# Holding back the feed-forward weight loads of a decoder layer until a given load of the second output projection

## The chip, the cores and the metric

One core of one Trainium2 chip runs the whole program. The metric is the device time of one execution in microseconds (us); the time before is the median of three runs. Engines: PE is the matmul engine and PEld its weight load, DVE, ACT and POOL are the vector, scalar and GpSimd engines, and SP issues the DMAs.

## The reference

One decoder layer, batch 1, 1024 tokens, model width 1024, float32. The token mixer has two halves of 512 columns, an RWKV-7 recurrence over 8 heads and a causal convolution of width 31, from one input projection `w_in` to one output projection `w_out`. A gated feed-forward network with a causal convolution of width 3 and an inner width of 2816 follows.

```python
h = _rms_norm(x, norm_pre_mix)
p = h @ w_in                     # 2 x 512 convolution columns, then the RWKV columns
...                              # recurrence, head norm, gate; convolution, norm, silu
mix = jnp.concatenate([rwkv_out, c], axis=-1) @ w_out
x = x + _rms_norm(mix, norm_post_mix)
h = _rms_norm(x, norm_pre_ffn)
hid = _causal_dwconv(h @ ffn_up, ffn_conv_w, ffn_conv_b)
gate, up = hid[..., :D_FF], hid[..., D_FF:]
x = x + _rms_norm((gelu(gate) * up) @ ffn_down, norm_post_ffn)
```

## The kernel before

**Weights.** Every large product is done in three matmuls on a rounded high part and a low part: high by high, high by low and low by high. `Trunk.weight` makes such a pair. It loads a 128 x 512 block (256 KB) into a raw buffer `wr` on SP's queue (line 180), ACT rounds it to `wh` and POOL subtracts to get `wl` (both on line 166, a helper). Line 139 is the helper of every matmul and line 154 that of the transposes on PE, so tiles tell more than lines: `pb`, `pe`, `pc`, `xs` and `Y` are PSUM banks, `h` the normed input of the mixer in two parts, `f` that of the feed-forward network, `wm` a pair of `w_out`.

**Order.** The code is written as streams with priorities, and a scheduler puts each engine's instructions into one fixed order. An engine runs its own in that order, and an instruction that waits holds up all behind it. `weight` runs at high priority, so a load whose buffer is free goes to the front of the order. SP has eight DMA semaphores in turn: each DMA waits until the one eight before it has landed. `tc.issue_after(i)` allows the instruction inside it only behind instruction `i` in that order; the kernel has it in a few places.

**Raw buffers.** The feed-forward phase takes its raw buffers in turn from two pools: two from `wq`, then three from `wp`. Those of `wq` hold nothing in the mixer.

**Stages.** First the program loads rows of `x` (`l8`), `params` (370 columns of per-channel constants), and the `lora` weights. Each row block is normed (lines 302 to 323: a sum of squares on ACT, its root on POOL at line 161, the scaling on ACT and DVE), transposed on PE, and written as `h` with a per-channel factor out of `params` (ACT line 288, DVE line 290). The first projection follows. The sequence is done in two halves of 512 tokens, and the recurrence in four quarters. Between about 20 and 655 us projection, recurrence, convolution and nine early pairs of feed-forward columns run interleaved. `norm_ffn(0)` in that stretch makes `f` of the first half: a sum of squares on ACT into `pt` (line 880), a factor `kk` on DVE (line 887), matmuls of `kk` with the row, then ACT line 288 and DVE line 290. The recurrence of the same stretch inverts small triangular matrices in a chain on DVE (`sub` and `dw`, lines 602 and 604). The second output projection `w_out(1)` ends the mixer at about 675 us. It has four column blocks `ch` of 256, each with four loads `k2`. The rest is the feed-forward network.

Of the kernel before, what the change touches and what calls it, by code (L numbers as in the profile page):

```python
# [100 lines left out]
class Trunk:  # L101
    def __init__(self, ctx, tc, a):
        self.ctx, self.tc, self.nc, self.a = ctx, tc, tc.nc, a
        self.at = dict(PRIO)
        self.n = 0

        self.low_pool = True

        once = [None]
        self.homes = {"wr": cycle(once), "wh": cycle(once), "wl": cycle(once)}  # L110

    def nm(self, s):
# [61 lines left out]
    def weight(self, src, shape, home=None, held=None, kept=None):  # L174


        with self.tc.high_priority():
            raw = (self.f2p.tile(shape, F32, tag="f2", name=self.nm("wr")) if held is self.hp else
                   self.wtile("wr", shape))
            self.load = self.nc.sync.dma_start(raw, src)  # L180
            if held:
                hi, lo = self.pair("w", held)
            elif home:
                hi, lo = (home[0].tile(shape, F32R, tag=t, bufs=BUFS[t], name=self.nm("wm")) for t in home[1:])
            else:
                hi, lo = (self.wtile(t, shape, F32R) for t in ("wh", "wl"))
            if kept and kept[0]:
                self.nc.scalar.copy(hi, raw)  # L188
                self.nc.sync.dma_start(lo.bitcast(F32), kept[1])
            else:  # L190
                self.low = self.split(hi, lo, raw, self.low_pool)[1]
        if kept and not kept[0]:
            self.nc.sync.dma_start(kept[1], lo.bitcast(F32))
        return hi, lo
# [579 lines left out]
    def w_out(self, h, mixr, co, behind=None):  # L774
        nc = self.nc
        if h == 0:
            acts = self.pairs("m")
        else:
            acts = []
            for _ in range(2):  # L780
                two = [self.tl("l8", [P, 4, HALF], F32R) for _ in range(2)]
                acts += [tuple(b[:, k] for b in two) for k in range(4)]
        with ExitStack() as gate:
            if behind is not None:
                gate.enter_context(self.tc.issue_after(behind.ins))
            for k in range(KT):
                self.split(*acts[k], mixr[:, k] if k < 4 else co[k - 4])

        def evac(ch, pss, post):
            for b, ps in enumerate(pss):  # L790
                o = self.tl("t2", [P, 512])
                with self.tc.high_priority():
                    nc.vector.tensor_tensor(
                        o.rearrange("p (t c) -> p t c", t=2), ps.rearrange("p (t c) -> p t c", t=2),
                        post.unsqueeze(1).broadcast_to([P, 2, 256]), ALU.mult)
                    for t in range(2):
                        tt = 4 * h + 2 * b + t
                        c = slice(t * 256, (t + 1) * 256)
                        nc.scalar.activation(ps[:, c], ps[:, c], AF.Square, accum_out=self.ssq[:, tt, ch:ch + 1])  # L799
                r = h * HALF + b * 256  # L800
                nc.sync.dma_start(
                    self.mixd[r:r + 256, ch * 256:(ch + 1) * 256].rearrange("(t p) c -> p t c", t=2),
                    o.rearrange("p (t c) -> p t c", t=2))

        for ch in range(4):
            post = self.tl("po", [P, 256])
            nc.sync.dma_start(post, self.a["post_mix"][:, ch * 256:(ch + 1) * 256].broadcast_to([P, 256]))
            pss = self.xs if ch == 1 else [self.bank("pe" if h and ch == 2 else "pb") for _ in range(2)]
            for k2 in range(KT // 2):
                wh, wl = self.weight(self.a["w_out"][ch, k2], [P, 2, 256], (self.mix, "ca", "ck") if h else None)  # L810
                for t in range(4):
                    for kk in range(2):
                        k = 2 * k2 + kk
                        hi, lo = acts[k]
                        s = slice(t * P, (t + 1) * P)
                        out = pss[t // 2][:, (t % 2) * 256:(t % 2 + 1) * 256]
                        start = k == 0 and t % 2 == 0
                        i = self.mm(out, hi[:, s], wh[:, kk], start=start, stop=False, skip=True)
                        if start:
                            first = i  # L820
                        elif k == 0 and kk == 0:
                            self.after(i, first)
                        self.mm(out, hi[:, s], wl[:, kk], start=False, stop=False, skip=True)
                        self.mm(out, lo[:, s], wh[:, kk], start=False, stop=k == KT - 1, skip=True)
            evac(ch, pss, post)


    def setup_ffn(self, ctx):
# [429 lines left out]
    def mixer(self, sts):  # L1258
        nc, tc = self.nc, self.tc
        W = [None] * 4  # L1260
        mixes = [None] * 2
# [141 lines left out]
                nc.sync.dma_start(self.early[i], self.ffn_pair(0, h0, i, piece, two[:, i % 2 * HALF:(i % 2 + 1) * HALF]))  # L1403
        prepare(4)
        with self.stream("proj"):
            self.w_out(1, mixes[1], [sts[1]["co", i] for i in range(4)], W[3].merged)
        return h0


# [71 lines left out]
```

## Time and profile before

| | |
|---|---|
| median of 3 runs | 1265.08 us |
| lowest and highest | 1264.17 and 1265.79 us |
| profiled execution | 1266.88 us |
| its span | 1265.1 us |
| mean granted PE clock | 0.984 |
| PE busy | 1216.0 us of the span |
| DVE, ACT, POOL busy | 901.4, 730.6, 512.2 us |
| moved by DMA | 180.97 MB, mean 143 GB/s |

The profiled execution has its own time: 1.8 us lies around its span, and it stands 1.8 us above the median. "Idle" is time in which an engine has no instruction in flight, and the bracket at the end of a row gives the idle time ahead of it and what ended it. The granted clock of PE is given in tenths of full speed (9 in a slice is 90% or more) or as a mean.

### The profile page before, as it was taken

The numbers are of one execution on the slowest core, as the hardware profiler recorded it, in microseconds if no ns is written. First come the engines' busy times: TensorE is split into PE (matmuls) and PEld (weight loads), VectorE is DVE, ScalarE is ACT, GpSimd is POOL, SyncE is SP. The second block draws the span as 40 slices with busy tenths as digits, with TensorE's granted clock in tenths as the row PEclk, the third lists the DMA queues.
The fourth block names the chain that finished last, engine by engine and source line by source line (L and its number), as shares of the span: only waits on it lengthen the run. The fifth ranks groups of instructions, "written<-read, shape, count | busy, mean of one in ns | idle before, by whom it ended". The sixth has DMA issues, their size and how long they took to land.

```text
span 1265.1 us, 22976 instructions
## 1 busy us (share of the span) xinstructions
PE 1216.0 (96%) x8424; PEld 993.7 (79%) x8424; DVE 901.4 (71%) x1558; ACT 730.6 (58%) x1516; POOL 512.2 (40%) x447
## 2 busy tenths in 40 slices
PE   5999999999998998999999999999999999999997
PEld 4767777788777876778889888888888888888885
DVE  6275999798678978999640455666766669479668
ACT  6564564564954676465763476876556556545451
POOL 3443330002103332244464389998889860000002
PEclk9999997999999989999999999999999999999998
DMA  7644442344332354133354698995232335336413
GB/s 254 172 133 141 127 133 71 90 126 126 111 119 80 110 157 137 44 88 90 100 141 147 226 333 288 305 319 165 79 84 77 93 127 179 100 104 225 133 56 133
DMA packets 102912, 180.97 MB, mean 143 GB/s; under 512 B 14896, under 2 KB 21424, under 8 KB 102800
## 3 DMA queue, kind: packets, MB, share of 16 engines
q1 hardware_dynamic: 102800, 179.51, 45.2%
q8 instruction: 66, 1.08, 0.4%
q14 instruction: 46, 0.38, 0.1%
HBM read 138.44 MB, written 41.03 MB: 142 GB/s over the span
## 4 chain that ended last, share of the span: by engine, by line
PE 78%; DVE 10%; ACT 5%; issue 2%; DMA 2%; POOL 2%; SPq 0%; POOLq 0%; DVEq 0%; ACTq 0%
PE pb L139 39%; PE xs L139 17%; PE pe L139 16%; DVE pc L427 3%; PE Y L139 2%; PE pc L139 2%; POOL wl L166 1%; PE pe L154 1%; DVE dw L604 1%; DMA pt<-mixd 1%; DMA params<-params 1%; DVE pt L496 1%; PE pc L154 1%; DVE sub L602 1%; PE xs L154 0%
## 5 line engine op out<-in xcount | busy, mean ns | idle before, releaser
L166 POOL TENSOR_TENSOR wl<-wr,wh 128x512 fp32r<-128x512 f32 (+2 forms) x175 | 233.7, 1337 | 226.0 <-ACT wh L166 188.9
L139 PE MATMUL pb<-h,wh 128*128 128x512 f32 (+3 forms) x720 | 231.4, 402 | 2.1 <-ACT wh L166 1.4
L166 ACT CAST wh<-wr 128x512 fp32r<-128x512 f32 (+1 forms) x214 | 131.3, 615 | 132.8 <-PE pb L139 42.8
L139 PE MATMUL pb<-f,wh 128*128 128x512 f32 x648 | 203.2, 393 | 0.7 <-ACT pb L799 0.4
L427 DVE SCALAR_TENSOR_TENSOR pc<-c,params,pc 128x512 f32<-128x512 f32 x232 | 174.2, 751 | 7.5 <-ACT pc L424 3.4
L139 PEld LDWEIGHTS pb<-h,wh 128*128 128x128 f32 (+2 forms) x720 | 133.0, 191 | 34.8 <-ACT wh L166 3.3
L139 PE MATMUL pb<-h,wl 128*128 128x512 f32 (+3 forms) x360 | 146.6, 407 | 2.1 <-POOL wl L166 2.0
L139 PEld LDWEIGHTS pb<-f,wh 128*128 128x128 f32 x648 | 120.9, 188 | 26.1 <-issue 1.0
L139 PE MATMUL pb<-f,wl 128*128 128x512 f32 x324 | 128.0, 396 | 0.0
L161 POOL TENSOR_TENSOR ss<-var,mhalf 128x1 f32<-128x1 f32 x16 | 11.6, 732 | 222.7 <-DVE var L160 222.6
L1069 POOL TENSOR_TENSOR b<-b,b 128x512 f32<-128x512 f32 x72 | 93.4, 1300 | 2.0 <-DMA wr<-ffn_up 0.6
L139 PEld LDWEIGHTS pb<-h,wl 128*128 128x128 f32 (+2 forms) x360 | 68.6, 190 | 21.1 <-POOL wl L166 4.2
L139 PE MATMUL xs<-f,wh 128*128 128x512 f32 x240 | 74.1, 390 | 0.3 <-DVE act L966 0.3
L166 POOL TENSOR_TENSOR wl<-b,wh 128x512 fp32r<-128x512 f32 x48 | 67.1, 1398 | 13.4 <-ACT wh L166 11.6
L139 PEld LDWEIGHTS pb<-f,wl 128*128 128x128 f32 x324 | 60.8, 188 | 12.9 <-POOL wl L166 0.4
L139 PE MATMUL pe<-f,wh 128*128 128x512 f32 x208 | 64.1, 389 | 0.0
L166 ACT CAST wh<-b 128x512 fp32r<-128x512 f32 x48 | 29.7, 618 | 57.4 <-PE pb L139 17.1
L717 POOL TENSOR_TENSOR XG<-r,GE 64x256 f32<-64x256 f32 x30 | 20.6, 690 | 80.2 <-DVE r L736 58.9
L139 PEld LDWEIGHTS xs<-f,wh 128*128 128x128 f32 x240 | 44.9, 188 | 9.9 <-DVE act L966 0.8
L166 ACT CAST a<-act 128x512 fp32r<-128x512 f32 x50 | 30.0, 619 | 33.4 <-PE Y L139 18.9
L188 ACT CAST wh<-wr 128x512 fp32r<-128x512 f32 (+2 forms) x44 | 26.4, 603 | 37.5 <-PE pb L139 21.0
L166 ACT CAST w<-wr 128x512 fp32r<-128x512 f32 x38 | 23.5, 622 | 41.3 <-PE Y L139 20.0
(419 smaller groups left out, 2965.9 us busy)
## 6 DMA issues: line engine op xcount, KB each, us to landing
wr<-ffn_up SPq DMA_DIRECT2D x99, 256.0 KB, 3.3
wr<-w_in SPq DMA_DIRECT2D x80, 256.0 KB, 2.9
b<-ffn_up SPq DMA_DIRECT2D x52, 256.0 KB, 2.7
b<-ffn_down SPq DMA_DIRECT2D x44, 256.0 KB, 4.6
sums<-b SPq DMA_DIRECT2D x44, 256.0 KB, 4.0
wr<-sums SPq DMA_DIRECT2D x44, 256.0 KB, 2.8
lows<-wl SPq DMA_DIRECT2D x40, 256.0 KB, 3.3
wl<-lows SPq DMA_DIRECT2D x40, 256.0 KB, 2.7
```

Of the source, the lines that this page charges most:

```text
L139: return self.nc.tensor.matmul(out, lhsT, rhs, start=start, stop=stop, skip_group_check=skip)
L154: self.nc.tensor.transpose(out, in_, self.con("ident")[:n, :n])
L161: self.nc.gpsimd.tensor_tensor(out, v[:, :n], self.mhalf[:, :n], ALU.pow)
L166: return self.nc.scalar.copy(hi, src), eng.tensor_tensor(lo, src, hi.bitcast(F32), ALU.subtract)
L188: self.nc.scalar.copy(hi, raw)
L427: nc.vector.scalar_tensor_tensor(out, c[:, j:j + HALF], w(j), acc, ALU.mult, ALU.add)
L496: nc.vector.tensor_tensor_scan(sg[:, l], self.con("scan"), sg[:, l], 0.0, ALU.mult, ALU.add)
L602: nc.vector.tensor_tensor(tv, dv[:, j + 1:, j:j + 1].broadcast_to([P, n, j]), dv[:, j:j + 1, :j].broadcast_to([P, n, j]), ALU.mult)
L604: nc.vector.tensor_tensor(dv[:, j + 1:, :j], dv[:, j + 1:, :j], tv, ALU.add)
L717: nc.gpsimd.tensor_tensor(x[64:128], R[64:128, gs], w.GE[64:128, c, gs].unsqueeze(2).broadcast_to([64, 4, CH]), ALU.mult)
L1069: sub = lambda o, x, y, op=ALU.subtract: self.nc.gpsimd.tensor_tensor(o, x, y, op)
```

## The change

`weight` gets a gate: once `self.start` is set, each of its loads may stand only behind that instruction. `w_out` keeps the load that its second column block begins with, and the mixer sets `self.start` to that of the second output projection. The loads of the mixer itself, of `w_out` and of the nine early pairs are made while `start` is still `None`; all loads that `weight` makes later are of the feed-forward network.

```diff
@@ Trunk.__init__
+        self.start = None
@@ Trunk.weight
-            self.load = self.nc.sync.dma_start(raw, src)
+            with ExitStack() as gate:
+                if self.start is not None:
+                    gate.enter_context(self.tc.issue_after(self.start.ins))
+                self.load = self.nc.sync.dma_start(raw, src)
@@ Trunk.w_out
                 wh, wl = self.weight(self.a["w_out"][ch, k2], ...)
+                if ch == 1 and k2 == 0:
+                    mark = self.load
...
+        return mark
@@ mixer
-            self.w_out(1, mixes[1], [sts[1]["co", i] for i in range(4)], W[3].merged)
+            self.start = self.w_out(1, mixes[1], [sts[1]["co", i] for i in range(4)], W[3].merged)
```

On SP at the start of the program, three loads of `ffn_up` stand among the first loads before. Behind the rows of `x`, SP has before:

```order
L302 DMA l8_4_129<-x 128x512 x4
L180 DMA wr_1194_7921<-ffn_up 128x512
L180 DMA wr_1197_7940<-ffn_up 128x512
L213 DMA params_78<-params 128x370
L214 DMA const_79<-consts 128x449
L244 DMA lora_106<-lora 96x512
L248 DMA wr_1_109<-lora 128x512
L248 DMA wr_2_113<-lora 128x512
L180 DMA wr_46_274<-w_in 128x512
L302 DMA mixr_111_679<-x 128x512 x4
L302 DMA ck_112_680<-x 128x512
L180 DMA wr_1219_8045<-ffn_up 128x512
```

and now:

```order
L306 DMA l8_4_129<-x 128x512 x4
L217 DMA params_78<-params 128x370
L218 DMA const_79<-consts 128x449
L248 DMA lora_106<-lora 96x512
L252 DMA wr_1_109<-lora 128x512
L252 DMA wr_2_113<-lora 128x512
L184 DMA wr_46_274<-w_in 128x512
L306 DMA mixr_111_679<-x 128x512 x4
L306 DMA ck_112_680<-x 128x512
L306 DMA ck_113_681<-x 128x512
```

The three loads are gone from there. With them the split of the first leaves ACT (`wh_1195`) and POOL (`wl_1196`): on POOL it stood ahead of the root of the last row block. Before:

```order
L161 TENSOR_TENSOR ss_32_212<-var_35_218,mhalf_83 128x1
L166 TENSOR_TENSOR wl_1196_7924<-wr_1194_7921,wh_1195_7923 128x512
L161 TENSOR_TENSOR ss_36_223<-var_38_229,mhalf_83 128x1
L251 TENSOR_TENSOR lw_108<-wr_1_109,lw_108 32x512
L251 TENSOR_TENSOR lw_108<-wr_2_113,lw_108 32x512
```

and now:

```order
L162 TENSOR_TENSOR ss_32_212<-var_35_218,mhalf_83 128x1
L162 TENSOR_TENSOR ss_36_223<-var_38_229,mhalf_83 128x1
L255 TENSOR_TENSOR lw_108<-wr_1_109,lw_108 32x512
L255 TENSOR_TENSOR lw_108<-wr_2_113,lw_108 32x512
L167 TENSOR_TENSOR wl_48_277<-wr_46_274,wh_47_276 128x512
```

The root `ss_36` now follows the one before it at once. At the second output projection ACT's casts of the feed-forward weights stand elsewhere. Before:

```order
L166 CAST wm_1112_7403<-wr_1111_7401 128x512
L166 CAST l8_1100_7319<-co_902_6129 128x512
L166 CAST wh_1198_7942<-wr_1197_7940 128x512
L923 ACT_TABLE_LOAD
L923 ACTIVATE pt_1068_6992<-pt_1068_6992 128x512
L166 CAST wm_1115_7433<-wr_1114_7431 128x512
L903 ACTIVATE pt_1076_7034<-pb_1069_6997,params_78 128x512
L905 COPY ecarry_93<-pb_1069_6997 128x2
L166 CAST wm_1121_7475<-wr_1120_7473 128x512
```

and now:

```order
L167 CAST wm_1112_7403<-wr_1111_7401 128x512
L930 ACT_TABLE_LOAD
L930 ACTIVATE pt_1068_6992<-pt_1068_6992 128x512
L167 CAST wm_1115_7433<-wr_1114_7431 128x512
L910 ACTIVATE pt_1076_7034<-pb_1069_6997,params_78 128x512
L912 COPY ecarry_93<-pb_1069_6997 128x2
L167 CAST wm_1121_7475<-wr_1120_7473 128x512
L167 CAST wh_1195_7923<-wr_1194_7921 128x512
L167 CAST wh_1198_7942<-wr_1197_7940 128x512
L167 CAST wm_1124_7505<-wr_1123_7503 128x512
```

Here `wr_1120` is the load that the gate names, and the two casts `wh_1195` and `wh_1198` have moved behind its cast; on SP the loads `wr_1194` and `wr_1197` follow `wr_1120` directly.

The order in the middle of the mixer is not the same either, though no line of its code is changed. On all engines it is the same from about row 50 up to the work that runs at about 170 us before, and again from the end of `w_out(1)`; between, the scheduler has placed many instructions a few rows up or down, and ACT has one table load fewer in all. The place of the largest shift that the prediction speaks of is `norm_ffn(0)` next to the recurrence, on ACT. Before:

```order
L590 COPY l8_792_5305<-l8_792_5305 32x32x32
L288 ACTIVATE f_880_5988<-pb_887_6019,params_78 128x256
L288 ACTIVATE f_882_5990<-pb_887_6019,params_78 128x256
L726 COPY r_833_5518<-xs0_100 64x256
L567 COPY ck_809_5431<-pe_808_5426 128x512
L567 COPY ck_811_5438<-pe_810_5433 128x512
L880 ACTIVATE pt_894_6050,sf_858_5939<-row_892_6044 128x512
L726 COPY r_833_5518<-xs1_101 64x256
L567 COPY ck_813_5445<-pe_812_5440 128x512
L567 COPY ck_815_5452<-pe_814_5447 128x512
```

and now:

```order
L887 ACTIVATE pt_894_6050,sf_858_5939<-row_892_6044 128x512
L292 ACTIVATE f_880_5988<-pb_887_6019,params_78 128x256
L292 ACTIVATE f_882_5990<-pb_887_6019,params_78 128x256
L594 COPY l8_792_5305<-l8_792_5305 32x32x32
L730 COPY r_833_5518<-xs0_100 64x256
L730 COPY r_833_5518<-xs1_101 64x256
L571 COPY ck_809_5431<-pe_808_5426 128x512
L571 COPY ck_811_5438<-pe_810_5433 128x512
L292 ACTIVATE f_868_5976<-pb_896_6060,params_78 128x256
```

The last sum of squares `pt_894` stands six rows higher, and the factors of `f` behind it (`f_868`) follow before `ck_813`. On DVE the second half of `f` stands now ahead of most of the chain of `sub` and `dw`:

```order
L606 TENSOR_TENSOR sub_818_5467<-dw_103 128x26
L608 TENSOR_TENSOR dw_103<-dw_103,sub_818_5467 128x13x2
L294 SCALAR_TENSOR_TENSOR f_869_5977<-pb_896_6060,params_78,f_868_5976 128x256
L294 SCALAR_TENSOR_TENSOR f_871_5979<-pb_896_6060,params_78,f_870_5978 128x256
L740 TENSOR_TENSOR r_843_5829<-xs0_100,XG_844_5838 64x256
L606 TENSOR_TENSOR sub_819_5470<-dw_103 128x36
```

Before, `f_869` stood three steps of that chain later, behind the `dw` of `sub_821`.

## Prediction

> **What bounds the kernel now.** I read the busy lines and the clock of the page first, then busy time by stretch, for where PE has time to win.
>
> ```profile
> PE 1216.0 (96%) x8424; PEld 993.7 (79%) x8424; DVE 901.4 (71%) x1558; ACT 730.6 (58%) x1516; POOL 512.2 (40%) x447
> PEclk9999997999999989999999999999999999999998
> 0.00:20.00 20.00, 7.85 (x30) 5.58 (x31) 11.41 (x34) 13.51 (x30) 8.21 (x15) 1.00 0.89 296
> 20.00:40.00 20.00, 18.48 (x88) 15.09 (x87) 9.74 (x29) 11.56 (x25) 7.82 (x10) 1.00 0.51 170
> 300.00:340.00 40.00, 39.62 (x305) 30.99 (x304) 27.82 (x55) 28.81 (x58) 6.51 (x10) 1.00 0.36 112
> 480.00:500.00 20.00, 17.21 (x218) 14.63 (x218) 17.66 (x43) 12.05 (x30) 4.73 (x6) 0.91 0.45 150
> 500.00:520.00 20.00, 16.52 (x110) 13.01 (x106) 17.45 (x52) 10.43 (x24) 2.89 (x5) 0.91 0.05 16
> 640.00:660.00 20.00, 18.83 (x125) 17.07 (x124) 11.48 (x14) 14.55 (x29) 15.47 (x12) 1.00 0.58 151
> 720.00:1240.00 520.00, 520.00 (x2311) 430.44 (x2310) 353.99 (x552) 313.50 (x639) 277.40 (x217) 1.00 0.52 168
> ```
>
> In the rows of stretches the columns are start and end, length, then busy time of PE, PEld, DVE, ACT and POOL, the granted clock, and the DMA engines' share and GB/s. PE is the bound: from 720 to 1240 us it has no idle time, and its order there is unchanged, so nothing can be won or lost in that stretch. PE is idle for 12.15 us at the start, where the DMA engines are 89% busy, 1.52 us in the next 20, 1.17 us around 650, and 6.3 us from 480 to 520, at a lower clock. The change touches these places.
>
> **The start.** Here is the chain of work that ended last for the first 30 us (start, length, what), then rows of the timeline, then two of the DMA view of the first 26 us.
>
> ```profile
> 4.97 0.57 SPq L180
> 6.20 7.10 DMA params<-params
> 13.32 5.39 DMA mixr<-x
> 18.77 4.99 DMA wr<-w_in
> 23.79 0.63 ACT wh L166
> 24.48 1.28 POOL wl L166
> 25.80 5.95 PE pb L139 x34
> ```
>
> ```profile
> 11.56 0.62 ACT L166 CAST wh<-wr 128x512 fp32r<-128x512 f32 x1 [0.33 <-DMA wr<-ffn_up]
> 12.61 1.28 POOL L166 TENSOR_TENSOR wl<-wr,wh 128x512 fp32r<-128x512 f32 x1
> 13.39 0.84 ACT L288 ACTIVATE h<-pe,params 128x256 fp32r<-128x256 f32 x2
> 13.84 0.79 POOL L161 TENSOR_TENSOR ss<-var,mhalf 128x1 f32<-128x1 f32 x1
> 21.18 0.77 PE L139 MATMUL pb<-h,wh 128*128 128x256 f32 x2 [0.48 <-DVE h L290]
> 24.46 0.80 PE L139 MATMUL pb<-h,wh 128*128 128x256 f32 x2 [0.38 <-ACT wh L166]
> 25.80 0.58 PE L139 MATMUL pb<-h,wl 128*128 128x256 f32 x1 [0.55 <-POOL wl L166]
> 28.74 0.63 PE L139 MATMUL pb<-h,wh 128*128 128x256 f32 x2
> 29.78 0.40 PE L139 MATMUL pb<-h,wh 128*128 128x256 f32 x2
> 15.40 0.33 SPq L180 DMA_DIRECT2D wr<-ffn_up  x1
> 31.66 0.62 ACT L166 CAST wh<-wr 128x512 fp32r<-128x512 f32 x1 [0.82 <-PE pb L139]
> ```
>
> ```profile
> GB/s 0 0 32 158 334 321 277 303 265 221 277 202 230 388 407 403 398 405 358 232 286 271 347 388 391 384 384 391 391 378 391 388 355 347 383 397 375 224 69 3
> wr<-ffn_up SPq DMA_DIRECT2D x3, 256.0 KB, 6.6
> ```
>
> The chain runs through the first of two `ffn_up` issues ahead of `params`, then through transfers that queue behind each other, to the second `w_in` pair, for which PE waits twice: 0.38 us for `wh` at 24.46 and 0.55 us for `wl` at 25.80. The GB/s row cuts those 26 us into 40 slices, and from the 23rd on it stands at about 388. A load of 256 KB (0.262 MB) takes 0.262 / 388 GB/s = 0.68 us of that.
>
> The change removes two loads ahead of `params` and a third, issued at 15.40, ahead of the second `w_in` load. So `params` lands 2 x 0.68 = 1.35 us sooner, and that `w_in` block 3 x 0.68 = 2.0 us, since each DMA of SP waits for one that landed earlier by as much. ACT starts on `h` 0.1 us after `params` at 13.39; it loses the 0.62 us cast at 11.56, and POOL the 1.28 us subtraction, behind which the root at 13.84 had waited. ACT is busy from there to the first projection, so I take only the 0.62 us cast for the start of PE: 21.18 becomes 20.6. Both waits for the second pair then vanish, because `wl` is ready at 25.76 - 2.0 = 23.7, before PE asks at 25.80 - 0.60 - 0.38 - 0.55 = 24.27. The work that starts at 25.80 starts 1.53 us sooner.
>
> One price is not in the trace: PE runs at half rate here (0.63 us for two matmuls at 28.74, 0.40 us at 29.78, while the clock column says 1.00). If the full rate comes at the same moment as before, nothing is added. If it comes about 4 us after the last stall, as before (25.80 to 29.4), with no stall after 20.6 it comes at about 24.6, and the 4.8 us until 29.4 shrink by half, 2.4 us. I add 0.9 of that, below the middle because the DVE chain at 21 us may stall PE again: 2.4 us for the start, with bounds 0.6 (only the cast goes) and 3.9.
>
> [...]
>
> **The second output projection.** Two casts move on ACT, and three loads on SP's queue, into this stretch.
>
> ```profile
> 649.58 0.63 ACT L166 CAST wh<-wr 128x512 fp32r<-128x512 f32 x1
> 652.72 0.38 PE L139 MATMUL pb<-wm,l 128*128 128x256 f32 x1 [0.31 <-ACT wm L166]
> 653.96 0.50 PE L139 MATMUL xs<-wm,l 128*128 128x256 f32 x2 [0.86 <-ACT wm L166]
> 654.30 7.25 PE L139 MATMUL pb<-wm,l 128*128 128x256 f32 x59
> ```
>
> ACT is the engine that PE waits for, 0.31 + 0.86 us. The cast of `wh_1198` at 649.58 lies in ACT's chain ahead of those waits and moves behind `wm_1121`, a gain of up to 0.63 us. Against that, `wm_1124` now has two casts of 0.63 us ahead of it, and these wait for loads issued only behind `wr_1120`. PE then has 7.25 us of matmuls, from 654.30 on, that need none of them, and the loads, 3 x 0.68 us, fill a queue that is 58% busy. SP's two later `ffn_up` loads wait for a buffer that POOL frees, with `w_out` loads queued behind; those have the same cover. I take a gain of 0.3 us, bounds -0.6 and +1.3 (both casts exposed).
>
> **The middle.** The gate moves nothing there itself, but the scheduler's order changed with the times it assumes. Most of it lies where PE has nothing to win: from 300 to 340 us, where ACT loses a table load, PE is idle for 0.38 us of 40. I put this at nothing, covered by PE's own queue; its bound is one half-clock stretch of 3.4 us either way, 1.7 us. The largest shift is in `norm_ffn(0)`.
>
> ```profile
> 501.69 0.27 PE L139 MATMUL xs<-r,ck 128*64 128x64 f32 x1 [1.17 <-ACT r L726]
> 502.62 0.65 ACT L880 ACTIVATE pt<-row 128x512 f32<-128x512 f32 x1
> 505.75 0.28 DVE L887 TENSOR_SCALAR kk<-const,sf 128x128 f32<-128x128 f32 x1
> 510.25 3.30 PE L139 MATMUL pb<-kk,row 128*128 128x128 f32 x16 [2.03 <-DVE sub L602]
> 513.78 0.89 PE L139 MATMUL pb<-f,wh 128*128 128x512 f32 x2 [0.23 <-DVE sub L602]
> 509.24 0.87 DVE L290 SCALAR_TENSOR_TENSOR f<-pb,params,f 128x256 fp32r<-128x256 f32 x2
> 518.81 1.16 DVE L612 STREAM_TRANSPOSE dw<-dw 64x512 f32<-64x512 f32 x1
> ```
>
> The chain is `pt` at 502.62, `kk` at 505.75, PE, then the four `f` pairs of DVE, the first at 509.24, for which PE's second batch waited 2.03 us; the `sub` named there stood ahead on the same engine. From 513.78 on PE has feed-forward work in plenty. ACT's `pt` now stands ahead of two `f`, two `ck` copies and a copy of `r`, about 2.5 us sooner, so PE's waits of 1.17, 2.03 and 0.23 us, together 3.4 us, can be filled by recurrence work that stood ahead of them. I take half, 1.7 us, because that work depends on ACT and DVE too. Bounds: 3.4 gained, plus one half-clock stretch that ends with the idle, 1.7, so 5.1; or as much as 3.5 lost, below.
>
> **The sum.** The profiled execution took 1266.88 us (span 1265.1). 2.4 + 0.3 + 1.7 = 4.4 us gives 1262.5 for it. It stands 1.8 us above the median of 1265.08, so I forecast 1260.7.
>
> **Rivals.**
>
> *Gained at the start, given back (within 0.2%, 2.5 us, which is about what a measurement of this kernel can tell from no change).* The shift of 1.5 us arrives at a stage that waits for something else. For it speaks the idle time of PE at 480 to 520 us, where DVE is busy for 17.66 and 17.45 us of 20 and could be the one that sets the pace; against it, that work on the weights, such as the cast at 31.66, is released by PE itself and shifts along. Start 1.5, middle nothing: 1265.1 - 1.5 = 1263.6.
>
> *Slower by the inversion.* On DVE eight `f` of 0.44 us (0.87 for two) now stand ahead of the chain of `sub` and `dw` that ends in the transpose at 518.81. If PE and ACT are late with the second batch, DVE waits at these `f` and the chain ends later by 3.5 us and more. It decides from the point at which PE runs out of feed-forward matmuls behind 513.78. Then PE waits 3.5 us, one half-clock stretch adds 1.7, and a second one elsewhere in the reordered mixer 1.7 more: 1265.1 - 2.4 + 6.9 = 1269.6, or 1267.9 without the last.
>
> *Faster by the start alone.* The clock comes early, the middle stays as it is: 1265.1 - 3.9 + 0.3 = 1261.5 to 1262.
>
> *The gate stalls the transition.* ACT waits at `wh_1195` for its load and PE runs dry before `wm_1124`: +1.3 us, 1263.8 with the start's gain. PE's 7.25 us of cover speak against it.
>
> **Chances.** The sum 0.40 and the start alone 0.14, so 0.54 faster; given back 0.19 and stalled transition 0.06, so 0.25 the same; the inversion or its like 0.21 slower. The range takes in the start at its bound with the middle at its own (1265.1 - 3.9 - 0.6 - 4 = 1256.6) and above it the inversion at its lower price: 1256.5 to 1267.5. That leaves out a fifth: the inversion's dearer half and the sums of all the best bounds.
>
> **What would show it.** In the changed kernel `params` should land near 12 us, the first projection start near 20.6, PE show no wait for the second `w_in` pair, and two matmuls of 128x256 fall to 0.40 us near 25 to 28 instead of 29.6. At 640 to 660 PE should wait less than 1.17 us, with `wm_1124` cast before PE needs it. At 500 to 520 PE should be busy for more than 16.52 us. If PE's time at the end of `w_out(1)` is not 3 us or more sooner, the middle took the gain; a longer chain of `sub` and `dw` with PE waiting for `dw` behind it would be the inversion.

## The result, and the profile after

The changed kernel takes 1253.91 us (median of six runs, 1252.75 to 1257.58) against 1265.43 us of the kernel before beside it (1264.06 to 1266.73): a ratio of 0.9913 with an interval of 0.9897 to 0.9929, 11.5 us faster. The forecast was 1260.7 us, and its range ended at 1256.5. The profiled execution took 1257.58 us, the slowest of the six, with a span of 1255.8 us; against the profiled one of before, 1265.1 us, it shows 9.3 of the 11.5 us.

These are the busy line, the clock line and the stretches of the changed kernel, with the columns as in the prediction.

```profile
PE 1210.4 (96%) x8424; PEld 988.9 (79%) x8424; DVE 899.8 (72%) x1558; ACT 729.1 (58%) x1515; POOL 507.1 (40%) x447
PEclk9999998999999989999999999999999999999999
0.00:20.00 20.00, 8.46 (x32) 5.98 (x32) 11.00 (x36) 13.50 (x31) 6.81 (x14) 1.00 0.90 299
20.00:40.00 20.00, 18.79 (x99) 14.76 (x99) 8.58 (x27) 11.46 (x25) 9.15 (x10) 1.00 0.52 152
300.00:340.00 40.00, 39.04 (x278) 29.86 (x277) 29.50 (x56) 32.27 (x67) 6.75 (x11) 1.00 0.39 118
428.00:455.00 27.00, 25.61 (x340) 23.37 (x339) 26.12 (x41) 19.42 (x49) 10.81 (x10) 1.00 0.47 134
480.00:500.00 20.00, 16.91 (x175) 13.22 (x173) 19.28 (x50) 16.52 (x40) 3.61 (x6) 1.00 0.20 70
500.00:520.00 20.00, 19.57 (x312) 15.86 (x314) 19.07 (x39) 8.54 (x16) 7.06 (x6) 0.91 0.19 48
640.00:660.00 20.00, 20.00 (x166) 19.91 (x165) 3.73 (x5) 9.20 (x22) 14.49 (x11) 0.99 0.75 220
720.00:1240.00 520.00, 520.00 (x2311) 430.70 (x2310) 353.63 (x560) 306.11 (x623) 276.17 (x216) 1.00 0.51 164
```

The stretch of 428 to 455 us was not shown of before; it is there:

```profile
428.00:455.00 27.00, 22.91 (x340) 20.82 (x339) 25.08 (x40) 19.17 (x41) 7.07 (x7) 0.89 0.44 113
```

PE is idle there for 4.09 us before and 1.39 us after, and the granted clock goes from 0.89 to 1.00. From 720 us on nothing has changed, as forecast. Stretches by the clock hide a shift, because work has moved against them. So the table takes one PE matmul, the same in both kernels, at each of ten places, and gives how much sooner (minus) it starts than in the kernel before; the first line is its time before. It is worked out from the traces.

| us before | 40 | 272 | 380 | 392 | 410 | 428 | 455 | 527 | 639 | 663 |
|---|---|---|---|---|---|---|---|---|---|---|
| changed kernel | -3.4 | -4.5 | -4.1 | -2.9 | -5.7 | -6.4 | -12.9 | -13.7 | -12.6 | -9.3 |
| `start_only` | -1.4 | -1.1 | -1.1 | -1.1 | -1.1 | -1.1 | -2.0 | -3.6 | -4.1 | -4.7 |
| `order_only` | -1.2 | -2.3 | -2.0 | -0.7 | -3.5 | -4.2 | -10.8 | -12.4 | -12.9 | -9.8 |
| `stage3a` | -1.8 | -3.3 | -3.3 | -3.3 | -3.3 | -4.0 | -11.3 | -9.8 | -9.8 | -10.3 |
| `pool_slot` | -1.2 | -1.1 | -1.1 | -1.1 | -3.8 | -3.8 | -3.8 | -4.7 | -4.8 | -5.5 |
| `evac_pe` | -2.0 | -2.0 | -2.0 | -2.0 | -2.0 | -2.0 | -7.3 | -5.2 | -5.0 | -5.8 |
| `combo` | -2.1 | -4.0 | -4.0 | -4.0 | -6.7 | -7.4 | -14.7 | -16.6 | -17.2 | -14.6 |

In the changed kernel 3.4 us are won by 40 us, 2.8 from 392 to 410, 6.5 from 428 to 455, and 3.3 are lost from 639 to 663. The two gains in the middle stand at places to which the prediction gave nothing. One trace is one execution, and the start differs by 1.3 us among kernels with one order there (in the eight gated ones with the old order the first 128x512 matmul starts at 28.87 to 30.18 us); the verdicts below go by medians.

### The profile page after: what moved, and what is told of

Its sections match the earlier page's. It is cut to its first block, busy times and chain, and to the rows that moved or that the text cites. A ratio compares the mean times of both kernels' runs of the same rounds, so it can differ in the third digit from the quotient of the medians.

```text
span 1255.8 us, 22979 instructions
## 1 busy us (share of the span) xinstructions
PE 1210.4 (96%) x8424; PEld 988.9 (79%) x8424; DVE 899.8 (72%) x1558; ACT 729.1 (58%) x1515; POOL 507.1 (40%) x447
## 4 chain that ended last, share of the span: by engine, by line
PE 62%; DVE 6%; ACT 2%; issue 1%; DMA 1%; POOL 1%; POOLq 0%; DVEq 0%; ACTq 0%
PE pb L140 27%; PE xs L140 16%; PE pe L140 14%; PE Y L140 2%; PE pc L140 2%; DVE pc L431 2%; DMA pt<-mixd 1%; PE pc L155 1%; PE pe L155 0%; DVE x L1120 0%; DVE m L167 0%; DVE sub L606 0%; DVE nrow L1136 0%; DVE dw L608 0%; DVE t L797 0%
## 5 line engine op out<-in xcount | busy, mean ns | idle before, releaser
L167 POOL TENSOR_TENSOR wl<-wr,wh 128x512 fp32r<-128x512 f32 (+1 forms) x175 | 230.0, 1316 | 219.4 <-ACT wh L167 191.3
```

The source lines that it names most:

```text
L167: return self.nc.scalar.copy(hi, src), eng.tensor_tensor(lo, src, hi.bitcast(F32), ALU.subtract)
```

## The experiments

**How an order is held.** The change does two things: it takes three loads out of the start, and the scheduler, which then counts with other times, puts hundreds of instructions of the mixer elsewhere. To part them, most kernels below carry a written table of each engine's instructions and force that order:

```python
def in_order(tc, nc, table):
    at = {i.name: i for i in nc.cur_bb.bb.instructions}
    edge = lambda: mybir.DependencyInfo(mybir.DependencyClass.NoSync, mybir.DependencyReason.DATA)
    for row in table:
        for p, q in zip(row, row[1:]):
            tc.add_manual_dep(at[f"I-{q}"], f"I-{p}", edge(), reason="in_order")
```

"The old order" is that of the kernel before, "the new order" that of the changed one; the four feed-forward blocks that the gate itself moves are left out of the table, so that they stand where the gate or its absence puts them. Every ratio is against the kernel before, run beside it on the same chip.

### The gate and the order apart: `start_only` and `order_only`

```diff
 # start_only: the gate as in the changed kernel
-        Trunk(ctx, tc, a).run()
+        Trunk(ctx, tc, a).run(), in_order(tc, nc, OLD_ORDER)
 # order_only: without the gate, the loads at the start
-        Trunk(ctx, tc, a).run()
+        Trunk(ctx, tc, a).run(), in_order(tc, nc, NEW_ORDER)
```

> The gate as in the changed kernel, but every engine's instructions other than those of the first four feed-forward blocks are held in the order of the kernel before by a written table. Theory A (the start is worth its own 3.4 us, the new order of the mixer the rest): about 1262. Theory B (the start is everything, the mixer only follows): about 1254. Theory C (neither is worth anything without the other): about 1265.

> No gate: the feed-forward loads stand at the start as before, but every other instruction is held in the order of the changed kernel by a written table. Theory A: the order is worth what the start is not, 1265.4 - 8.1 = about 1257. Theory B: 1265. Theory C: 1265 or slower, because that order was made for the earlier start.

`start_only` took 1263.73 us against 1264.44, a ratio of 0.9995 (0.9986 to 1.0003): no difference that can be told. `order_only` took 1256.77 us, 0.9938 (0.9919 to 0.9957), with the three loads still ahead of `params`. So the order alone carries 7.7 us of the 11.5, and taking the loads away, with nothing else moved, at most about 1.8 (1264.44 x 0.0014). Theory A had 1257 and 1262 for these two: the order came as it said, the start fell 1.7 us short. With the new order the loads are worth more: from 0.9938 to the changed kernel's 0.9913, some 3 us, though these intervals overlap.

The start of the changed kernel and of `start_only`, rows of the timeline:

```profile
12.02 0.84 ACT L292 ACTIVATE h<-pe,params 128x256 fp32r<-128x256 f32 x2 [0.99 <-PE pe L155]
20.42 0.77 PE L140 MATMUL pb<-h,wh 128*128 128x256 f32 x2 [0.48 <-DVE h L294]
22.48 0.46 PE L140 MATMUL pb<-h,wh 128*128 128x256 f32 x2
23.95 0.39 PE L140 MATMUL pb<-h,wl 128*128 128x256 f32 x1 [0.66 <-POOL wl L167]
```

```profile
12.17 0.72 ACT L326 ACTIVATE l<-l,ss 128x512 f32<-128x512 f32 x1 [1.82 <-POOL ss L162]
12.80 0.82 ACT L292 ACTIVATE h<-pe,params 128x256 fp32r<-128x256 f32 x2
20.57 0.76 PE L140 MATMUL pb<-h,wh 128*128 128x256 f32 x2 [0.48 <-DVE h L294]
24.11 0.58 PE L140 MATMUL pb<-h,wl 128*128 128x256 f32 x1 [0.21 <-POOL wl L167]
```

In the changed kernel `h` begins at 12.02 instead of 13.39 us, the projection at 20.42 instead of 21.18, and the wait for the second pair shrinks from 0.38 + 0.55 to 0.66 us. These are the forecast's landmarks, but the loads alone do not give them. The order differs at the start too. In the old order ACT's scaling `l` of the last row block stands ahead of `h`, in the new one behind it. In the kernel before, `h` follows straight upon this `l`:

```profile
12.67 0.72 ACT L322 ACTIVATE l<-l,ss 128x512 f32<-128x512 f32 x1 [0.49 <-POOL ss L161]
```

In `start_only` the `l` waits 1.82 us for POOL's root `ss`, and `h` behind it begins at 12.80.

The 14 gated kernels of this study, one trace of each, fall in two groups by this. In the eight with the old order at the start `h` begins at 12.80 to 14.11 us and the projection at 21.12 on average, no sooner than the 21.18 of the kernel before. In the six with `h` ahead of `l` these are 11.77 to 12.58 and 20.63. The first 128x512 matmul of the next block starts at 29.43 us on average in the eight and 28.75 in the six, 29.14 in all; in the kernel before, `order_only` and `moves_no_gate` it starts at 31.58, 29.82 and 32.00. So about 2 us are won there, though the 29.82 lies among the gated ones. The eight then wait 0.66 to 0.68 us for the `wl` of that block, which the changed kernel does not. By 40 us they are 1.3 us ahead of the kernel before on average, and the six 2.5 us. By these averages about half of the gain at the start hangs on the order.

### Does the place matter that the gate names? `gate_early` and `gate_lora`

```diff
 # gate_early: the gate names the last load of w_in for the v and g columns (about 100 us)
+        late = self.load
-            self.start = self.w_out(1, ...)
+            self.w_out(1, ...)
+        self.start = late
 # gate_lora: the gate names the last of the two lora loads at the start
-            nc.sync.dma_start(raw, a["lora"][:, e])
+            self.pl = nc.sync.dma_start(raw, a["lora"][:, e])
+        self.start = self.pl
```

> The gate names another load, the last of the v and g columns of the input projection at about 100 us, and the rest of the order comes out as in the changed kernel but for a few rows. If it matters only that the loads leave the start: about 1254, as the changed kernel. If the named place, the second output projection, matters: off by 2 us or more, slower because three loads now share the queue with the projection's.

> The gate names the last load of the small lora weights at the start, so that two of the three feed-forward loads stand four places later than in the kernel before, still ahead of the first block of the input projection, and one behind that projection's third block; the scheduler gives a third order, which differs from both others in the mixer in about as many rows as they do from each other. If only the loads leaving the start counted: about 1264. If the order of the mixer counts and is not tied to the loads: anywhere from 1252 to 1270, and its profile differs from the others between 170 and 660 us by more than at the start.

`gate_early` took 1253.83 us, 0.9919 (0.9906 to 0.9932): as fast as the changed kernel, though its loads may come 500 us sooner. The scheduler gives it the new order of the mixer but for a few rows. So it does not matter that the gate names the second output projection. `gate_lora`, which only keeps the loads behind those of `lora`, gets a third order and is slower: 1268.27 us, 1.0027 (1.0014 to 1.0039). Against the same matmuls of before it lost 5.6 us between 620 and 644 us, of which 1.7 came back by 655:

```profile
620.00:640.00 20.00, 16.87 (x84) 13.79 (x84) 13.72 (x21) 16.90 (x31) 7.54 (x7) 0.98 0.37 105
640.00:660.00 20.00, 19.63 (x109) 16.95 (x109) 6.62 (x9) 8.56 (x18) 13.74 (x11) 0.85 0.58 158
639.68 1.22 PE L140 MATMUL pb<-f,wh 128*128 128x512 f32 x2 [3.13 <-ACT wh L167]
```

PE is idle for 3.13 us of the first stretch, all of it in one wait for the `wh` of an early pair, and runs at a clock of 0.85 in the second. The same kind of edit can lose as well as win, by the order that comes with it.

### Where in the order: `start_stage3`, `stage3a`, `stage3b`, `late_before`

All four have the gate. They take the new order for one part of the program and the old one for the rest.

```diff
-        Trunk(ctx, tc, a).run()
+        Trunk(ctx, tc, a).run(), in_order(tc, nc, MIXED)
 # start_stage3: new from 416 to 528 us     stage3a: new from 416 to 471 us
 # stage3b:      new from 471 to 528 us     late_before: new up to 528 us
```

> The gate, and the order of the changed kernel only between about 416 and 528 us of the kernel before (the stretch with the norm of the feed-forward rows beside the recurrence); the order before elsewhere. By the profiles of the two kernels PE gained 6.7 us in that stretch. Theory A: 1265.4 - 3.4 - 6.7 = about 1255 if that stretch's order carries it and nothing is given back; 1258 if the 3.1 us that the changed kernel lost again at about 635 us come too. Theory B: 1254 whatever the order. Rival within A (the gain of that stretch is only the arrival time from earlier stretches): about 1262.

> The gate, and the order of the changed kernel only from about 416 to 471 us of the kernel before (the second input projection of the convolution beside the recurrence's inversion); the order before elsewhere. If the waits of the recurrence and the half-rate stretch that follows them at 449 to 456 us are what the new order removes: about 1259, and PE's idle time in the stretch from 428 to 455 falls from 4.1 to about 1.4 us. If that stretch only shifts a wait to the next: about 1263.7, as with the start alone.

> The gate, and the order of the changed kernel only from about 471 to 528 us (the norm of the feed-forward rows beside the recurrence, the place that the prediction priced at 1.7 us). By that price 1263.7 - 1.7 = 1262. If the whole of the gain between 416 and 528 us sits here: 1258. If it needs the earlier arrival from the stretch before: 1263.7.

> As the changed kernel up to about 528 us, and in the order of the kernel before from there on. The changed kernel loses about 3 us at 634 us where PE waits for the last early pair's weights; if the order behind 528 us makes that loss, about 1251; if it comes from arriving earlier, 1254; if the order behind 528 us was itself a gain elsewhere, 1256.

| | median, us | ratio | interval |
|---|---|---|---|
| `start_stage3` | 1258.22 | 0.9955 | 0.9940 to 0.9970 |
| `stage3a` | 1257.39 | 0.9944 | 0.9931 to 0.9956 |
| `stage3b` | 1263.78 | 0.9991 | 0.9982 to 1.0000 |
| `late_before` | 1255.66 | 0.9932 | 0.9918 to 0.9946 |

The stretch of 416 to 471 us carries 0.9995 - 0.9944 = 0.0051, some 6.4 us, by itself. That of 471 to 528, in which `norm_ffn(0)` lies, carries nothing: `stage3b` stands where `start_only` stands, and `start_stage3`, with both parts, is no faster than `stage3a`. The traces of `start_only` (first two rows) and of `stage3b` (third) say why.

```profile
507.27 2.04 PE L140 MATMUL pb<-kk,row 128*128 128x128 f32 x16 [2.03 <-DVE sub L606]
510.33 0.70 PE L140 MATMUL pb<-f,wh 128*128 128x512 f32 x2 [1.02 <-DVE sub L606]
523.89 1.89 PE L140 MATMUL pe<-l,dw 32*16 32x16 f32 x128 [2.69 <-ACT dw L636]
```

The two waits for `sub` are gone in `stage3b`. PE comes sooner to its feed-forward matmuls, runs out of them, and waits 2.69 us for the `dw` at the end of the inversion. Between the same matmuls of 471 and 527 us it is idle for 7.79 us against 7.67 in `start_only`: the wait has moved. `start_stage3` and `late_before`, which have the old order behind 528 us, show that wait too, 2.66 us in each. The changed kernel does not, but by the table it wins nothing from 455 to 639 us either (-12.9 to -12.6).

`late_before` holds the larger part of the gain, and what the new order does behind 528 us is not told apart from nothing, by overlapping intervals. In its trace the loss of the changed kernel from 639 to 663 us is absent (-11.6 to -12.3), yet its time is nearest to the 1256 of its expectation's third case, not to the 1251 of the first.

What happens from 440 us on is seen in the timelines. In the kernel before, ACT and then PE:

```profile
446.00 0.37 ACT L799 ACTIVATE pb<-pb 128x256 f32<-128x256 f32 x1
446.50 0.62 ACT L662 COPY l<-l 64x512 f32<-64x512 f32 x1
447.51 0.61 ACT L662 COPY l<-l 64x512 f32<-64x512 f32 x1
448.15 1.09 ACT L518 ACTIVATE pt<-pt,ka 128x256 f32<-128x256 f32 x2
449.54 0.36 ACT L799 ACTIVATE pb<-pb 128x256 f32<-128x256 f32 x1
447.17 0.34 PE L139 MATMUL xs<-r,l 128*64 128x64 f32 x4 [1.10 <-ACT l L662]
448.18 0.57 PE L139 MATMUL xs<-r,l 128*64 128x64 f32 x12 [0.68 <-ACT l L662]
449.69 0.58 PE L139 MATMUL pe<-lx,lw 96*128 96x256 f32 x1 [0.94 <-ACT l L658]
450.67 0.63 PE L139 MATMUL pb<-wh,m 128*128 128x256 f32 x2
```

and in `stage3a`:

```profile
439.14 0.37 ACT L803 ACTIVATE pb<-pb 128x256 f32<-128x256 f32 x1
440.46 0.37 ACT L803 ACTIVATE pb<-pb 128x256 f32<-128x256 f32 x1
440.85 1.08 ACT L522 ACTIVATE pt<-pt,ka 128x256 f32<-128x256 f32 x2
441.95 0.62 ACT L666 COPY l<-l 64x512 f32<-64x512 f32 x1
441.00 0.39 PE L140 MATMUL pb<-wh,m 128*128 128x256 f32 x1 [0.52 <-ACT pb L803]
441.34 0.40 PE L140 MATMUL pb<-wh,m 128*128 128x256 f32 x2
```

The first output projection, `w_out(0)`, fills one bank, ACT reads it twice (line 799 before, 803 now, a square sum for each half), and the next column block can then start in that bank. Before, the second reading stands at 449.54, behind copies for the recurrence (line 662) and `pt` (line 518). PE has 24 matmuls of the next block in hand, but ahead of them in its own order stand nine instructions of the recurrence which wait for the same copies: 1.10, 0.68 and 0.94 us. Then it runs at half rate, 0.63 us for two matmuls at 450.67. In the new order ACT has read twice by 440.83 us (440.46 + 0.37), PE waits 0.52 us, takes the 24 matmuls at full rate (0.40 us for two at 441.34) and does the nine behind them. The changed kernel itself has the same picture, with that 0.52 us at 439.38. From 428 to 455 us `stage3a` wins 7.3 us: PE's idle time falls from 4.09 to 1.09 us, 3.0 us, and its busy time for the same work from 23.1 to 18.8 us, 4.3 us. The half rate makes some 2.8 of these 4.3 by my estimate: before, the granted clock is 0.50 from 449.31 us on, 5.69 us of it ahead of 455, of which I take half, while it is 1.00 in all of that stretch in `stage3a`. The rest was not taken apart.

### Those two moves alone: `two_moves`, `evac_pe`, `evac_only`

The gate, the old order, and in it only the two moves. On ACT, `pb_755` is the bank in question.

```diff
 # PE (two_moves and evac_pe; evac_only leaves PE as it was)
-  xs<-r,l x8, pe<-lx,lw        ahead of the 24 matmuls pb<-wh,m / wl,m
+  xs<-r,l x8, pe<-lx,lw        behind them
 # ACT, two_moves: second reading three rows sooner, ahead of pt (line 522)
 # ACT, evac_pe and evac_only: directly behind the first reading
-  pb (first), l<-l, dw<-pe, l<-l, pt x2, l<-pe, pb (second)
+  pb (first), pb (second), l<-l, dw<-pe, l<-l, pt x2, l<-pe
```

> The gate and the order of the kernel before, with two moves alone: on PE the 24 matmuls that begin the next column block of the first output projection (pb_772) stand ahead of eight matmuls of the recurrence and one small one for which PE waited at 448 to 450 us, and on ACT the last reading of the bank that those 24 need (pb_755) stands three rows earlier. If this place, its waits and the half-rate stretch behind them are what the stretch from 416 to 471 us gained: 1257 to 1258.5. If the gain needs the many other moves of that stretch: about 1263, or slower because the recurrence comes later by 24 matmuls, 2.6 us.

> As two_moves, but ACT's last reading of the bank (pb_755) stands directly behind its first reading, ahead of the two copies for the recurrence behind which it still stood there; PE then waited 2.70 us for it. If that reading, on the order of ACT, is what holds PE up: PE's wait falls under 1 us, no half-rate stretch follows, and the time is about 1258. If the recurrence's copies, now 0.4 us later, hold up the rest: 1262 to 1263.

> The same move on ACT alone; on PE the nine matmuls of the recurrence keep their place ahead of the 24. If both engines' orders have to fit: PE still waits for the recurrence's copies, 1.10, 0.68 and 0.94 us, and the time is about 1263.7, as with the start alone. If ACT's order alone carried it: 1258.

`two_moves` took 1263.02 us, 0.9985 (0.9977 to 0.9994): not told apart from `start_only`. The trace says why: PE still stood before the 24 matmuls for that reading.

```profile
448.14 0.39 PE L140 MATMUL pb<-wh,m 128*128 128x256 f32 x1 [2.70 <-ACT pb L803]
```

In `evac_pe`, with the reading moved all the way, that is:

```profile
445.00 0.38 PE L140 MATMUL pb<-wh,m 128*128 128x256 f32 x1 [0.96 <-ACT pb L803]
```

It took 1261.09 us, 0.9969 (0.9958 to 0.9981), where 1258 was expected, and `evac_only` 1263.99 us, 0.9988 (0.9979 to 0.9997). So the reading alone brings nothing that can be told from `start_only`: in its trace PE still waits 1.60, 0.68 and 0.94 us for the recurrence ahead of those matmuls. The move on PE without the one on ACT was not run. Both moves together bring 2.9 us over `evac_only`, a little under half of what `stage3a` wins. In its trace `evac_pe` wins 5.3 us from 428 to 455 us and gives 2.1 back by 527. What brings the rest in `stage3a` is among the other moved rows of 416 to 471 us and was not parted further, so this place is shown as a whole and explained in a little under half.

### A subtraction of 4.9 us on POOL: `pool_slot`

This is POOL, DVE and PE of the kernel before at 399 us; the row of POOL is from the chain of work that ended last, the rest from the timeline.

```profile
399.01 4.90 POOL wl L166
398.90 0.67 DVE L166 TENSOR_TENSOR m<-mixr,m 128x512 fp32r<-128x512 f32 x1
399.50 1.27 DVE L166 TENSOR_TENSOR m<-co,m 128x512 fp32r<-128x512 f32 x2
400.71 0.74 DVE L427 SCALAR_TENSOR_TENSOR pc<-c,params,pc 128x512 f32<-128x512 f32 x1
401.50 1.27 DVE L166 TENSOR_TENSOR m<-co,m 128x512 fp32r<-128x512 f32 x2
403.36 0.61 DVE L602 TENSOR_TENSOR sub<-dw 128x56 f32<-128x56 f32 x1
403.95 0.51 PE L139 MATMUL pb<-wl,m 128*128 128x256 f32 x2 [2.15 <-POOL wl L166]
```

The subtraction that makes `wl` takes 1.28 us elsewhere (12.61 us, in the prediction) and 4.90 here, beside DVE's subtractions `m`, and PE waits 2.15 us for it. `pool_slot` has the gate, the old order and one move: DVE's product `pc` goes ahead of the three `m`.

```diff
 # DVE
-  sub, m<-mixr, m<-co, m<-co, pc, dw
+  sub, pc, m<-mixr, m<-co, m<-co, dw
```

> The gate and the order of the kernel before, with one move on DVE: a multiply-add of the convolution (pc) stands ahead of three subtractions (m) instead of behind them, at 399 to 401 us. POOL's subtraction that starts there took 4.9 us in the kernel before against 1.3 us for others of its kind, and PE waited 2.15 us for it. If DVE's run of subtractions holds POOL off: POOL's falls to under 2 us and PE's wait to under 0.5 us, about 1261.7 in all. If POOL's long time has another cause: it stays at 4.9 us, and the time at 1263.7.

It took 1260.91 us, 0.9973 (0.9964 to 0.9982), 2.8 us under `start_only`. Its timeline:

```profile
397.86 1.27 POOL L167 TENSOR_TENSOR wl<-wr,wh 128x512 fp32r<-128x512 f32 x1 [6.14 <-ACT wh L167]
397.76 0.74 DVE L431 SCALAR_TENSOR_TENSOR pc<-c,params,pc 128x512 f32<-128x512 f32 x1
398.42 1.26 DVE L167 TENSOR_TENSOR m<-mixr,m 128x512 fp32r<-128x512 f32 x1
399.74 0.50 PE L140 MATMUL pb<-wh,m 128*128 128x256 f32 x2 [1.46 <-DVE m L167]
```

POOL takes 1.27 us, and now the first `m`, which begins 0.56 us behind it, takes 1.26 instead of 0.67. PE waits 1.46 us, for `m`, where under 0.5 was expected. By the same matmuls the stretch of 392 to 410 us is 2.7 us shorter, 0.9 of it idle time (2.47 to 1.57). The rest, 1.8 us, is a faster PE: before, the granted clock is 0.50 for 3.41 us from 404.94 on (0.64 us for two matmuls at 405.05), which by half of that I estimate to cost 1.7 us, and in `pool_slot` it is 1.00 there (0.40 us for two). In the changed kernel POOL starts 0.14 us ahead of a `pc` of DVE, near the end of the `m` before it, and takes 1.37 us:

```profile
397.69 1.37 POOL L167 TENSOR_TENSOR wl<-wr,wh 128x512 fp32r<-128x512 f32 x1 [8.91 <-ACT wh L167]
```

The changed kernel wins 2.8 us there, in other parts: its idle time falls by 2.2 us, from 2.47 to 0.24, while a half-clock stretch of 3.41 us (from 391.23 on) stays. Together, `stage3a` at 0.9944 and the 0.0022 of `pool_slot` over `start_only` make 0.9922, which lies within the changed kernel's interval. This is a sum; no run holds just these two.

### The loss at the end of the mixer: `late_swap`

In the changed kernel, ACT casts one `wm` of the second output projection and rounds four `co` before it casts the `wh` of the last early pair, and PE runs out of work:

```profile
631.97 2.19 ACT L167 CAST l<-co 128x512 fp32r<-128x512 f32 x4
634.05 0.63 ACT L167 CAST wh<-wr 128x512 fp32r<-128x512 f32 x1
634.74 0.73 PE L140 MATMUL pb<-f,wh 128*128 128x512 f32 x2 [1.70 <-ACT wh L167]
636.39 0.50 PE L140 MATMUL pb<-f,wl 128*128 128x512 f32 x1 [0.92 <-POOL wl L167]
```

```diff
 # new order, ACT; POOL's wl likewise goes ahead of wm
-  wm<-wr, l<-co x4, wh<-wr
+  wh<-wr, wm<-wr, l<-co x4
```

> The changed kernel, with ACT's rounding and POOL's subtraction of the last early feed-forward block (wh_1074, wl_1075) moved ahead of the first weights of the second output projection and of the four casts of the convolution's half. In the changed kernel PE waited 1.70 and 0.92 us for these two at 634 to 636 us and ran at half rate behind. If that order makes the wait: about 3 us less than the changed kernel, 1251. If the weights of the second output projection are then late by as much: 1254, no change.

It took 1255.63 us, 0.9928 (0.9913 to 0.9942), no better than the changed kernel: the second case of the expectation, though not for its reason. The two waits, 2.62 us, are gone, and one has come in their place:

```profile
637.86 13.24 PE L140 MATMUL pb<-wm,l 128*128 128x256 f32 x96 [3.46 <-DVE pt L919]
```

PE comes sooner to a bank that DVE has yet to empty. The wait had only moved.

### What the runs point to: `moves_no_gate` and `combo`

`moves_no_gate` leaves the gate out and keeps the moves of `evac_pe` and `pool_slot` in the old order. `combo` is the changed kernel with the old order from 272 to 416 us and the moves of `pool_slot` and `late_swap`.

```diff
-        Trunk(ctx, tc, a).run()
+        Trunk(ctx, tc, a).run(), in_order(tc, nc, MOVES_IN_OLD)   # moves_no_gate, no gate
+        Trunk(ctx, tc, a).run(), in_order(tc, nc, COMBO)          # combo, with the gate
```

> The kernel before, without the gate and with its loads at the start, with the moves of evac_pe and of pool_slot alone: 24 matmuls on PE, one reading on ACT, one multiply-add on DVE. If these two places carry most of what the change gained: 1264.5 - 2.8 - 5.5 = about 1256, and the gate is not needed. If the gain of evac_pe does not come: about 1262.

> The changed kernel with the order of the kernel before from 272 to 416 us (where it had 1.9 us of idle time at 380 to 392 against 4.6), the move of pool_slot in that stretch, and the move of late_swap. If these add up: 1251 less about 1, 1250. If the stretch's own gain of the new order (1.2 us) is lost as well: 1251 to 1252.

`moves_no_gate` took 1260.99 us, 0.9967 (0.9955 to 0.9980): 4.3 us from eleven moved instructions (nine on PE, one each on ACT and DVE), with every load where it was. The expectation had 1256, with 5.5 us for the moves of `evac_pe`. By the runs above, `pool_slot` and `evac_pe` over `evac_only`, 2.8 + 2.9 = 5.7 us would have been left, and whether the two fully add up is not told by these intervals. `combo` took 1252.50 us, 0.9906 (0.9894 to 0.9919), the lowest median of all, 1.4 us under the changed kernel (0.9 by the ratios), though the intervals overlap; 1250 to 1252 was expected. Its trace shows what was meant: the 1.2 us that the new order loses from 380 to 392 us are not lost, and 2.7 are won from 392 to 410.

## Why the prediction was wrong

**The step that failed** is the one on the middle: "Most of it lies where PE has nothing to win: from 300 to 340 us, where ACT loses a table load, PE is idle for 0.38 us of 40. I put this at nothing, covered by PE's own queue". The order had changed in the whole mixer, and I took one well-filled stretch for all of it. At 392 to 410 us PE is idle for 2.47 us before, and at 428 to 455 for 4.09 us at a clock of 0.89. A walk through all stretches would have shown this idle time. The new order wins 2.8 and 6.5 us there, which is more than the 4.4 us of the whole sum. The bound of 1.7 us, half a stretch at half rate (3.41 us from 404.94 on in the trace of before), was too narrow as well: a reordered queue took away 3.0 us of idle time and 4.3 us of busy time in one place.

**The start**, -2.4 us. The landmarks came in the changed kernel: the projection at 20.42 us against 20.6, `h` at 12.02. The wait for the second pair did not vanish but shrank to 0.66 us. The prediction read `h` at 13.39 as released by `params`; in that trace `h` stands straight behind `l`, without a wait, and `l` had waited 0.49 us for POOL's root. With that order kept `h` came at 12.80 in `start_only`, so the landmarks needed ACT's new order, which the prediction did not count: their agreement is partly luck. With the old order the term measured 0.7 us (interval -0.4 to 1.8), and some 3 us with the new order around it. As a term of this change its size was about right; as a forecast of "the start alone", which that rival put at 1261.5 to 1262, it was too high, for `start_only` took 1263.7. The full rate was forecast for 24.6 us and came at 22.6 in the changed kernel, but between 22.6 and 26.7 from one gated kernel to the next.

**`norm_ffn(0)`**, -1.7 us. The rows did move, and PE's waits for `sub` are gone, as forecast, but `stage3b`, which moves them with the other rows of 471 to 528 us, wins nothing beyond `start_only` (1263.78 against 1263.73). What stands in their place is the sign that the prediction gave for the rival "slower by the inversion": PE waits 2.69 us for `dw` behind the chain. The price of that rival, 3.5 us and half rate on top of the waits as they were, did not come; the old waits and the new one about cancel. PE was busy for 19.57 us from 500 to 520, more than 16.52 as the prediction asked, but that work had come some 13 us sooner, so the sign says nothing of this place. I had chosen it because the shift in the order was largest there, not because an early release at that place was the one that ended PE's wait.

**The second output projection**, -0.3 us. The waits for `wm` at 640 to 660 us, together 1.17, are gone, as forecast, and PE is busy for all 20 us. Ahead of that stretch a new wait of 2.62 us stands, on the last early pair, and the same matmuls lose 3.3 us from 639 to 663. `late_swap` shows that taking it away exposes the next wait, so it has no price by itself. That the gate names this projection made no difference (`gate_early`).

**The rival "given back"** is what the change is without its order: `start_only` is within 0.2% of before. **The test that I set** told it: PE at the end of `w_out(1)` should be 3 us sooner or more, and it is 9.3 us sooner, but by the middle.

## What to carry to other kernels

When a scheduler makes the order, an edit to loads is also an edit to every queue, and the order has to be priced over the whole program: go through all stretches in which the bound engine is idle or at half rate, and ask at each which instruction ends the wait and whether it has moved. To learn what an edit is worth, run it in the old order and run the new order without it; here these gave 0.7 and 7.7 us of 11.5, the remainder being no more than their intervals leave open, and a sister edit with another order lost 3.5 us. Two small things are worth looking for: a reading that frees a bank, queued behind work that PE does not need yet (moved together with PE's own order, 2.9 us here), and a POOL operation that starts into a run of DVE operations (4.90 us here, and 1.27 with one DVE operation moved).

## What was not expected of the hardware

A POOL subtraction `wl`, about 1.3 us elsewhere (the median of 175 in a trace is 1.29 to 1.30, and no other is above 1.87), took 4.88 to 4.90 us in seven of the eight traces that have the old order of DVE there, and 3.27 us in the eighth (`start_stage3`). In the kernel before it began 0.11 us after a DVE subtraction that had more of its kind behind it. It took 4.90 - 1.27 = 3.6 us longer than in `pool_slot`, through several DVE operations (398.90 to 403.97 us). By what means DVE's order lengthens it was not shown. In `pool_slot`, where POOL began 0.56 us ahead of `m`, it took 1.27 us, and `m` 1.26 instead of 0.67; in the kernel before, where `m` began first, it took 4.90.

PE's full rate at the start (0.40 us for two 128x256 matmuls) came 2.1 us after the first projection in the changed kernel and 8.2 us after it in the kernel before, while the granted clock reads 1.00 there. That 1.00 is for want of a record: the clock's records begin at 22.59 us in the changed kernel and at 29.47 in the kernel before, where the full rate begins. In `evac_pe`, which has earlier records, the column reads 0.50 from 17.1 to 23.9 us; there two such matmuls take 0.63 us at 23.33 and 0.39 at 24.38. In the traces of the kernel before and of the changed kernel the half-clock stretches last 3.41 us (four in each), 6.83 (one) and 13.65 (one), but for the last, of 8.85 and 6.43 us, which runs past the program's end; at a granted clock of 0.50 I estimate that 3.41 us cost a busy PE half of that, 1.7 us of work. The full rate at the start came between 22.6 and 26.7 us in the gated kernels; half of that spread of 4.1 us, some 2 us, is my estimate of how much of an edit's effect there it can hide.
